# One decoder layer on one core: the program's work in program order, weight splits in pieces between matmul groups, attention over the full array

## The chip, the cores and the metric

The kernel runs on one core of a Trainium2 chip. A core has a matrix engine (TensorE, PE in the profile; its weight loads are shown as PEld), three engines for elementwise work (VectorE or DVE, ScalarE or ACT, GpSimd or POOL) and queues that issue DMAs, most of them on SyncE (SP). Each engine has its own stream of instructions, and waits on semaphores that others raise.

The metric is the time of one execution on the device in microseconds; lower is better. Three runs of the kernel before gave a median of 829.25 us (828.92 to 829.86).

## What is computed

One layer with 512 tokens of width 1024 and a memory of 256 rows, in float32. Each of three parts adds a normalised result to `x`:

```python
# 1. mixer: one input projection, 8 attention heads of 64 and 4 retention heads of 128
proj = rms_norm(x, pre_mix_g) @ w_in                     # 1024 -> 3584
a = dilated_attention(rope(aq), rope(ak), av)            # windows (128,1) (512,4) (2048,16)
a = a * rsqrt(mean(a * a) + eps) * attn_gn_g             # per head
r = retention(rope(rq), rope(rk) * 128 ** -0.5, rv)      # chunks of 128, decay by head
r = silu(rg) * (groupnorm(r) * ret_gn_g)
x = x + rms_norm(concat(a, r) @ w_out, post_mix_g)
# 2. cross attention on the memory, 4 heads of 256
q = rms_norm(x, pre_mem_g) @ w_q;  k, v = split(rms_norm(mem, mem_norm_g) @ w_kv)
x = x + rms_norm(softmax(q @ k.T / 16) @ v @ w_o, post_mem_g)
# 3. feed-forward, hidden 2816
g, u = split(rms_norm(x, pre_ffn_g) @ w_gate_up)
x = x + rms_norm((silu(g) * u) @ w_down, post_ffn_g)
```

## The kernel before

**Products.** Almost every product is made of three (`mm3`, lines 81 to 86): each operand is held as a high part rounded to TensorE's fast 32-bit format and the rest as a low part, and high x high, high x low and low x high are summed in PSUM. `split` (line 88) makes the two parts: ScalarE copies the high one, VectorE subtracts it for the low one.

**Weights.** They come in 67 blocks of 128 x 2048 (1 MB) in a fixed order: 14 of `w_in`, 8 of `w_kv`, 4 each of `w_out`, `w_q` and `w_o`, 22 of `w_gu` (gate and up), 11 of `w_dn`. `load` takes the next: a buffer `raw` (two of them), the DMA on SP's queue, then the split in halves of 1024 columns into `wh` and `wl`. `take` hands out a block and loads one or two ahead.

**Stages.** Queries and keys of the retention are projected feature by feature (`rqk`, eight PSUM banks at once) and rotated; then values and gate (`rv`, `rg`) block by block of tokens; then attention queries, keys and values (`aq`, `ak`, `av`) mixed with the retention's heads (`ret_inner`, `ret_state`, `ret_outer`). The eight attention heads follow: scores (`att_scores`, masked by a table that holds the logarithm of how often the three patterns see a key), transposes of the weights (`att_transposes`), values (`att_values`), a norm for each pair of heads (`att_norm`), with the projections of the memory (`mem_keys`, `mem_values`) as filler between them. Then the output projection (`mix_half`), the cross attention, its output projection by blocks of tokens (`mem_block`), gate and up (22 steps of 48 matmuls of 512 columns), and the down projection with the last residual.

**Order.** The kernel is written for a library that assigns buffers and semaphores. Without further options it also orders each engine's instructions itself, by priority and readiness. An instruction waits for the producers of what it reads, and for the readers of a buffer that it takes over.

In the scores, the first product of each pair holds all 128 rows of the array (`qk` holds a query's high half above its low half), the second only the 64 rows of the head, for the keys' low part:

```python
            nc.tensor.matmul(ps, lhsT=c, rhs=qk[pr][:, (2 + hh) * S:(2 + hh) * S + nn], start=True, stop=False)
            nc.tensor.matmul(ps, lhsT=c[rows], rhs=kl[rows, pr * S:pr * S + nn], start=False, stop=True)
```

The attention's values are products in full float32 with 64 output columns: four for a head, the two heads of a pair in the two halves of one bank.

Of the kernel before, what the change touches and what calls it, by code (L numbers as in the profile page):

```python
# [19 lines left out]
P = 128  # L20
# [18 lines left out]
def hybrid_layer(ctx, tc, t, out):  # L39
    nc = tc.nc  # L40
    cp = ctx.enter_context(tc.tile_pool(name="cp", bufs=1))
    up = ctx.enter_context(tc.tile_pool(name="up", bufs=20))
# [23 lines left out]
    def row(name):  # L66
        return wk.tile([P, D], F32, tag="w4k", name=uname(name), bufs=2)
# [31 lines left out]
    loaded = {}  # L99

    def load(pieces=1, swap=False):
# [3 lines left out]
        w = pair("w")  # L105
        n = 2048 // pieces
        for i in range(pieces):
            c = slice(i * n, (i + 1) * n)
            nc.sync.dma_start(raw[:, c], src[:, c])
        n = 2048 // max(2, pieces)  # L110
        for i in range(max(2, pieces)):
            c = slice(i * n, (i + 1) * n)
            if swap and i == 0:
                nc.vector.tensor_copy(w[0][:, c], raw[:, c])
                nc.vector.tensor_sub(w[1][:, c], raw[:, c], w[0][:, c].bitcast(F32))
            else:
                split(raw[:, c], w[0][:, c], w[1][:, c])
        loaded[key] = w

    def take(name, i, ahead=2):  # L120
        while (name, i) not in loaded:
            load()
        while chunks and len(loaded) - 1 < ahead:
            load()
        return loaded.pop((name, i))

    def ahead(name, i):
        while (name, i) in chunks:
            load()
# [35 lines left out]
    def load_gain(name):  # L165
        g = wk.tile([P, D], F32, tag="g", name=uname("g"), bufs=2)
        src = t[name]
        nc.sync.dma_start(g, bass.AP(tensor=src.tensor, offset=src.offset, ap=[[0, P], [1, D]]))
        return g
# [17 lines left out]
    def load_xT(k, between=None):  # L187
        raw = work("xraw")
        nc.sync.dma_start(raw, t["xT"][:, k, :])
        if between:  # L190
            between()
        split(raw, *hx(k, 0, S), gT[:, 0, k:k + 1])
# [6 lines left out]
    load_xT(0, lambda: load(4, True))  # L199
    load_xT(1)  # L200
    load_xT(2)
    load_xT(3)
    load(2)
    for k in range(4, KT):
        load_xT(k)
    load()
    x = load_rows("x")
    load()
    w_rqk = [take("w_in", i, 0) for i in range(4)]
    rope = unit("rope").rearrange("p (c s) -> p c s", c=4)  # L210
    nc.sync.dma_start(rope, t["rope"])
# [6 lines left out]
    pss = [bank("rqk") for _ in range(8)]  # L218

    def rqk(f, k):  # L220
        w = w_rqk[k // 2]
        mm3(pss[f], part(w, (k % 2) * D + f * P, P), hx(k, 0, S), k == 0, k == KT - 1)

    for k in range(4):
        for f in range(8):
            rqk(f, k)
    ahead("w_in", 4)
    rstd0 = row_rstd(x, TB, D, "r0")
    rbc = None
    for f in range(8):  # L230
        for k in range(4, KT):
            rqk(f, k)
        ps = pss[f]
# [19 lines left out]
    def tok_proj(c0, name, evict):  # L253
        ws = []

        def one(b):
            if b == 0:
                ws[:] = [take("w_in", c0, 1), take("w_in", c0 + 1, 2)]
# [3 lines left out]
            if b == TB - 1:  # L262
                ws.clear()
            evict(b, ps)
# [39 lines left out]
    off = [0, 512, 1024, 896]  # L304
# [64 lines left out]
    qk = [unit("qk", F32R) for _ in range(4)]  # L369
    kl = unit("kl", F32R)  # L370
    av = unit("av")
# [8 lines left out]
    def split_k(f, v):  # L380
        for i, (h, g) in enumerate(((ha, hb), (hb, ha))):
            o = qk[f][:, (2 + i) * S:(3 + i) * S]
            nc.scalar.copy(o[h], v[h])
            nc.vector.tensor_sub(kl[h, f * S:(f + 1) * S], v[h], o[h].bitcast(F32))
            nc.scalar.copy(o[g], o[h].bitcast(F32))

# [10 lines left out]
    def head_proj(c0, store, name):  # L397
        ws = {}

        def one(f):  # L400
# [4 lines left out]
            for k in range(KT):  # L405
                mm3(ps, part(w, k * 256 + (f % 2) * P, P), hx(k, 0, S), k == 0, k == KT - 1)
            t1, t2 = work("t1"), work("t2")
# [9 lines left out]

    def evict_av(b, ps):
        nc.scalar.mul(av[:, b * 512:(b + 1) * 512], ps, rstd0[:, b:b + 1])

# [7 lines left out]
    def att_scores(h):  # L428
        pr, hh = h // 2, h % 2
        rows = slice(hh * 64, hh * 64 + 64)  # L430
# [7 lines left out]
        for qb in (3, 2, 0, 1):  # L438
# [3 lines left out]
            ps = bk[sbank[qb][0]][:, sbank[qb][1]:sbank[qb][1] + nn]  # L442
            nc.tensor.matmul(ps, lhsT=c, rhs=qk[pr][:, (2 + hh) * S:(2 + hh) * S + nn], start=True, stop=False)
            nc.tensor.matmul(ps, lhsT=c[rows], rhs=kl[rows, pr * S:pr * S + nn], start=False, stop=True)
# [11 lines left out]

    def att_transposes(h):
        pt = pts.pop(h)
        u = unit("pT")
        bk = [bank("ptr") for _ in range(3)]  # L460
        for kb in (0, 1, 3, 2):
            ps = bk[off[kb] // 512]
            for qb in range(kb, TB):
                o = off[kb] % 512 + (qb - kb) * P
                nc.tensor.transpose(ps[:, o:o + P], pt[:, poff[qb] + kb * P:poff[qb] + (kb + 1) * P], ident)
        nc.scalar.copy(u[:, 0:512], bk[0])
        nc.vector.tensor_copy(u[:, 512:1024], bk[1])
        nc.scalar.copy(u[:, 1024:1280], bk[2][:, :256])
        pTs[h] = u

    def att_values(h):
        pr, hh = h // 2, h % 2
        rows = slice(hh * 64, hh * 64 + 64)
        if hh == 0:
            oTb[pr] = bank("oT")
        u = pTs.pop(h)
        for kb in range(TB):
            nc.tensor.matmul(oTb[pr][rows, kb * P:S], lhsT=av[:, kb * 512 + h * AD:kb * 512 + (h + 1) * AD],
                             rhs=u[:, off[kb]:off[kb] + S - kb * P], start=kb == 0, stop=kb == TB - 1)
        if hh == 1:  # L480
            ot = work("ot")
            nc.scalar.copy(ot, oTb.pop(pr))
            oTb[pr] = ot
# [27 lines left out]
    mem = {}  # L511

    def mem_prepare():
        raw = rawp.tile([P, KT, NM], F32, tag="raw", name=uname("memTr"))
# [7 lines left out]
    def mem_stats():  # L522
        mrow = rawp.tile([P, 2, D], F32, tag="raw", name=uname("mrow"))
# [5 lines left out]
    def mem_keys(f):  # L529
        if f % 2 == 0:  # L530
            mem["w"] = take("w_kv", f // 2, 1)
        ps = bank("mk")
        for k in range(KT):
            mm3(ps[:, :NM], part(mem["w"], k * 256 + (f % 2) * P, P), part(mem["T"], k * NM, NM), k == 0, k == KT - 1)
        kf = work("kf")
# [5 lines left out]
    def mem_values(c, b):  # L541
        if b == 0:
            mem["w"] = [take("w_kv", 4 + 2 * c + i, i) for i in range(2)]
        ps = bank("mv")
        for k in range(KT):
            mm3(ps, part(mem["T"], k * NM + b * P, P), part(mem["w"][k // 4], (k % 4) * 512, 512), k == 0, k == KT - 1)
        vf = work("vf")
        nc.scalar.mul(vf, ps, mem["r"][:, b:b + 1])
        hi, lo = part(mem["v"], b * D + c * 512, 512)
        nc.scalar.copy(hi, vf)  # L550
        nc.gpsimd.tensor_sub(lo, vf, hi.bitcast(F32))
# [49 lines left out]
    x = load_rows("x")  # L601
    g1 = load_gain("post_mix_g")
# [8 lines left out]
    ahead("w_out", 2)  # L611
    filler(9)
    att_out(3)
    w_out = {c: take("w_out", c, 0) for c in (2, 3, 0, 1)}

    def residual(pss, b, g, e=None, cuts=((0, 512), (512, 512))):
        e = e or nc.vector
        ss = small([P, len(cuts)], "ps")
        z = row("z")
# [12 lines left out]
    def normed(b, g, e=None):  # L632
        rs = row_rstd([x[b]], 1, D, "nr", e=e)
        h = row("h")
# [14 lines left out]
    def out_proj(bs, lhs, ws, ks, name, outer, mid=None):  # L649
# [11 lines left out]
        for b in bs:  # L661
            for n in range(2):
                if mid and (b, n) == (bs[-1], 1 if len(bs) == 1 else 0):
                    mid()
                for i in range(2 * outer, KT):
                    one(b, n, i)
        return pss
# [4 lines left out]
    g2 = load_gain("pre_mem_g")  # L672
# [3 lines left out]
    def mix_half(hf, mid=None):  # L676
        bs = (2 * hf, 2 * hf + 1)
        pss = out_proj(bs, y_lhs, w_out, order, "o1", 2, mid)
        hs = []
        for b in bs:  # L680
            e = nc.gpsimd if b == 3 else nc.vector
            residual(pss[b], b, g1, e)
            hs.append(normed(b, g2, e))
# [11 lines left out]
    wq = [take("w_q", c, 0) for c in range(4)]  # L695
    qT, pT, oT = {}, {}, {}

    def query(hf, f):
# [3 lines left out]
        for k in range(KT):  # L702
            mm3(ps[:, :256], part(wq[f // 2], k * 256 + (f % 2) * P, P), part(h2[hf], k * 256, 256), k == 0, k == KT - 1)
# [270 lines left out]
```

## Time and profile before

| what | value |
|---|---|
| median of three runs | 829.25 us |
| the profiled execution, first to last instruction | 828.5 us |
| its mean granted TensorE clock | 0.991 |
| DMA | 85.86 MB, mean 104 GB/s |
| HBM read, written | 83.11 MB, 2.10 MB |

Busy time of an engine is the union of its instructions. A matmul's row is longer than the distance to the next one, since its end is modelled and matmuls are pipelined; the distance between starts is what it takes of TensorE. The granted clock is the share of full speed that TensorE had. "Idle before" is the engine's idle time ahead of an instruction, and the arrow names what ended it. The page's chain covers 42% of the span with TensorE's matmuls, the down projection's and gate/up's groups at 5% each.

### The profile page before, as it was taken

To read this page: it belongs to the slowest core of one execution; us is meant where nothing else is said; L and a number is where in the kernel's file an instruction comes from. 1 tells how busy PE (TensorE), PEld (TensorE's weight loads), DVE (VectorE), ACT (ScalarE), POOL (GpSimd) and SP (SyncE) were. 2 spreads that over 40 slices of the span, in tenths; PEclk is the share of its full clock that TensorE was granted. 3 is DMA by queue.
4 is the path that set the end of the run, shared out by engine and by line. 5 is a ranking of instruction groups with operands and counts; after the bars stand their busy time and mean duration, and the time that the engine had idled before them with its cause. 6 is when DMAs were issued, how large, how long until landed. Compare 5 with 4: busy or idle time off the path is not lost. (4 is left out here: it accounts for less than half of the span.)

```text
span 828.5 us, 10220 instructions
## 1 busy us (share of the span) xinstructions
PE 807.9 (98%) x4108; PEld 675.7 (82%) x4108; DVE 396.6 (48%) x766; ACT 305.4 (37%) x537; POOL 132.8 (16%) x176
## 2 busy tenths in 40 slices
PE   9979999999999999999999899999999999999996
PEld 7768888877777878999988788888888888888884
DVE  5595168764565657758446441405050314222144
ACT  5504333466464733445435232222130305332110
POOL 0161024410110100300036300000000004236000
PEclk9998999999999999999999999999999999999998
DMA  8726212221124440524002340505050322521011
GB/s 305 291 77 236 94 51 87 73 95 52 51 70 175 163 153 0 197 109 153 1 1 102 127 153 1 203 1 203 1 203 1 121 82 74 182 102 51 1 51 51
DMA packets 15519, 85.86 MB, mean 104 GB/s; under 512 B 1904, under 2 KB 1904, under 8 KB 6896
## 3 DMA queue, kind: packets, MB, share of 16 engines
q1 hardware_dynamic: 14752, 84.16, 27.7%
q10 hardware_dynamic: 720, 1.06, 0.3%
q8 instruction: 32, 0.52, 0.3%
q14 instruction: 15, 0.12, 0.0%
HBM read 83.11 MB, written 2.10 MB: 103 GB/s over the span
## 5 line engine op out<-in xcount | busy, mean ns | idle before, releaser
L91 DVE TENSOR_TENSOR wl<-raw,wh 128x1024 fp32r<-128x1024 f32 (+1 forms) x135 | 166.5, 1267 | 102.6 <-ACT wh L90 70.2
L90 ACT CAST wh<-raw 128x1024 fp32r<-128x1024 f32 (+1 forms) x135 | 133.8, 1042 | 95.3 <-DMA raw<-in_w_in 38.1
L820 DVE TENSOR_TENSOR af<-sg,u 128x512 f32<-128x512 f32 x22 | 15.1, 686 | 133.7 <-PE u L86 133.7
L846 POOL TENSOR_TENSOR al<-af,ah 128x512 fp32r<-128x512 f32 x22 | 34.6, 1605 | 257.5 <-ACT ah L845 243.3
L84 PE MATMUL g<-h3h,wh 128*128 128x512 f32 (+1 forms) x192 | 72.1, 375 | 0.0
L84 PE MATMUL u<-h3h,wh 128*128 128x512 f32 (+1 forms) x192 | 71.7, 373 | 0.0
L85 PE MATMUL g<-h3l,wh 128*128 128x512 f32 (+1 forms) x192 | 71.3, 371 | 0.0
L86 PE MATMUL g<-h3h,wl 128*128 128x512 f32 (+1 forms) x192 | 71.3, 371 | 0.0
L85 PE MATMUL u<-h3l,wh 128*128 128x512 f32 (+1 forms) x192 | 71.3, 371 | 0.0
L86 PE MATMUL u<-h3h,wl 128*128 128x512 f32 (+1 forms) x192 | 71.3, 371 | 0.0
L84 PE MATMUL dn<-wh,ah 128*128 128x512 f32 x176 | 68.5, 389 | 0.0
L85 PE MATMUL dn<-wl,ah 128*128 128x512 f32 x176 | 68.5, 389 | 0.0
L86 PE MATMUL dn<-wh,al 128*128 128x512 f32 x176 | 68.5, 389 | 0.0
L817 ACT ACTIVATE sg<-g 128x512 f32<-128x512 f32 x22 | 13.1, 598 | 149.2 <-PE g L86 123.0
L84 PEld LDWEIGHTS g<-h3h,wh 128*128 128x128 f32 x192 | 36.5, 190 | 6.5 <-ACT h3h L90 0.2
L84 PEld LDWEIGHTS u<-h3h,wh 128*128 128x128 f32 x192 | 36.6, 191 | 6.3
L85 PEld LDWEIGHTS g<-h3l,wh 128*128 128x128 f32 x192 | 36.2, 188 | 6.4
L86 PEld LDWEIGHTS g<-h3h,wl 128*128 128x128 f32 x192 | 36.2, 188 | 6.2
L85 PEld LDWEIGHTS u<-h3l,wh 128*128 128x128 f32 x192 | 36.2, 188 | 6.2
L86 PEld LDWEIGHTS u<-h3h,wl 128*128 128x128 f32 x192 | 36.1, 188 | 6.1
L84 PEld LDWEIGHTS dn<-wh,ah 128*128 128x128 f32 x176 | 33.0, 188 | 6.9
L86 PEld LDWEIGHTS dn<-wh,al 128*128 128x128 f32 x176 | 33.0, 188 | 6.9
(267 smaller groups left out, 1752.8 us busy)
## 6 DMA issues: line engine op xcount, KB each, us to landing
raw<-in_w_gu SPq DMA_DIRECT2D x22, 1024.0 KB, 4.8
raw<-in_w_in SPq DMA_DIRECT2D x12, 1024.0 KB, 5.1
raw<-in_w_dn SPq DMA_DIRECT2D x11, 1024.0 KB, 4.7
raw<-in_w_kv SPq DMA_DIRECT2D x8, 1024.0 KB, 4.7
x<-in_x SPq DMA_DIRECT2D x4, 1024.0 KB, 10.2
raw<-in_w_out SPq DMA_DIRECT2D x4, 1024.0 KB, 5.3
raw<-in_w_q SPq DMA_DIRECT2D x4, 1024.0 KB, 5.3
raw<-in_w_o SPq DMA_DIRECT2D x4, 1024.0 KB, 4.7
```

Source lines behind the costliest of these rows:

```text
L84: nc.tensor.matmul(o, lhsT=sh, rhs=mh, start=start, stop=False)
L85: nc.tensor.matmul(o, lhsT=sh, rhs=ml, start=False, stop=False)
L86: nc.tensor.matmul(o, lhsT=sl, rhs=mh, start=False, stop=stop)
L90: nc.scalar.copy(hi, src)
L91: nc.vector.tensor_sub(lo, src, hi.bitcast(F32))
L817: nc.scalar.activation(sg, pg, AF.Silu)
L820: nc.vector.tensor_mul(af[-1][:, (f % 4) * S:(f % 4 + 1) * S], sg, pu)
L846: nc.gpsimd.tensor_sub(lo[:, c], af[i][:, c], hi[:, c].bitcast(F32))
```

## The change

- **Program order.** `TileContext` gets `linearize=True`. The instructions then stand on each engine in the order in which the code issues them.
- **Weights in pieces.** `load` becomes `fetch` (the DMA alone) and `piece` (one half of 1024 columns: ScalarE's high part, the low part on VectorE, or on GpSimd for the first halves of `w_kv` and `w_out`). The piece that completes a block also fetches the next. `bg` makes a piece if fewer than `ahead` blocks are ready, and stands in the code behind a matmul group and ahead of its eviction.
- **Start.** The transposed input and the first blocks of `w_in` are fetched and split between the groups of `rqk`.
- **Retention rotation.** ScalarE copies the two halves of the product in swapped places into `t2`, VectorE multiplies all 128 rows at once; before, VectorE multiplied each half into the other's place. The table's signs are exchanged to fit.
- **Attention.** The keys' low parts are held in both halves of the rows (one more copy, on GpSimd), so the second product of the scores uses all 128 rows. The transposed weights are split into high and low parts; the values are held as high and low parts side by side, 128 columns for a head; eight products in the fast format replace the four, and ScalarE and VectorE add the two halves of the result.
- **Buffers.** 23 units in place of 20; rows and gains come from units; a smaller scratch area for DMA descriptors.
- **Smaller ones.** `mem_values` takes one block at a time and keeps two banks; the memory's rows come into units; the last block of `mem_block` computes its norms on VectorE.

```diff
-    up = ctx.enter_context(tc.tile_pool(name="up", bufs=20))
+    up = ctx.enter_context(tc.tile_pool(name="up", bufs=23))
...
+    def fetch(pieces=1):
+        if not chunks:
+            return
         key = chunks.pop(0)
         src = t[key[0]][key[1]]
         raw = rawp.tile([P, 2048], F32, tag="raw", name=uname("raw"))
...
+    def piece(n=1024, first=False):
...
+        key, raw, w, c0 = e
+        c = slice(c0, c0 + n)
+        if first:
+            nc.vector.tensor_copy(w[0][:, c], raw[:, c])
+        else:
+            nc.scalar.copy(w[0][:, c], raw[:, c])
+        low = nc.gpsimd if key[0] in ("w_kv", "w_out") and c0 == 0 else nc.vector
+        low.tensor_sub(w[1][:, c], raw[:, c], w[0][:, c].bitcast(F32))
+        e[3] += n
+        ready[key] = w
+        if e[3] == 2048:
+            fetched.pop(0)
+            fetch()
+        return True
+
+    def bg(n=1, ahead=2):
+
+        for _ in range(n):
+            if fetched and (len(ready) - (fetched[0][0] in ready) < ahead):
+                piece()
...
+        nc.scalar.copy(t2[0:64], ps[64:128])
+        nc.scalar.copy(t2[64:128], ps[0:64])
         nc.vector.tensor_mul(t1, ps, rope[:, 0, :])
-        nc.vector.tensor_mul(t2[0:64], ps[64:128], rope[64:128, 1, :])
-        nc.vector.tensor_mul(t2[64:128], ps[0:64], rope[0:64, 1, :])
+        nc.vector.tensor_mul(t2, t2, rope[:, 1, :])
         nc.gpsimd.tensor_add(dst, t1, t2)
...
+            k0 = (pr % 2) * 2 * S + hh * S
             nc.tensor.matmul(ps, lhsT=c, rhs=qk[pr][:, (2 + hh) * S:(2 + hh) * S + nn], start=True, stop=False)
-            nc.tensor.matmul(ps, lhsT=c[rows], rhs=kl[rows, pr * S:pr * S + nn], start=False, stop=True)
+            nc.tensor.matmul(ps, lhsT=c, rhs=kl[pr // 2][:, k0:k0 + nn], start=False, stop=True)
...
+        for i, (c0, n) in enumerate(((0, 512), (512, 384), (1024, 384))):
+            split(bk[i][:, :n], hi[:, c0:c0 + n], lo[:, c0:c0 + n])
...
+        for kb, (c0, n, q0) in enumerate(pcol):
+            for i in range(2):
+                nc.tensor.matmul(ps[:, q0:q0 + n], lhsT=av_block(kb, h, 1), rhs=u[i][:, c0:c0 + n],
+                                 start=kb == 0 and i == 0, stop=kb == TB - 1 and i == 1)
         if hh == 0:
-            oTb[pr] = bank("oT")
...
+            oTb[pr] = work("ot")
+        ol = work("ol")
+        nc.scalar.copy(ol[ha], ps[hb])
+        nc.vector.tensor_add(oTb[pr][rows], ps[ha], ol[ha])
...
         for j, ps in enumerate((pg, pu)):
             for k in range(KT):
                 mm3(ps[:, c0:c0 + n], part(w, k * 256 + j * P, P), gx(k, c0, n), k == 0, k == KT - 1)
+            bg(1)
...
-    nc = _bacc.Bacc("TRN2", target_bir_lowering=False, num_devices=1)
+    nc = _bacc.Bacc("TRN2", target_bir_lowering=False, num_devices=1, dynamic_dma_scratch_size=1024)
...
-    with _tile.TileContext(nc) as tc:
+    with _tile.TileContext(nc, linearize=True) as tc:
```

How the instructions stand in the built programs, with the semaphores that each waits for (named by the engine or DMA queue that raises them), at three places.

ScalarE before, in the gate/up stage (`wh` is a weight block's high part, `sg` the gate after its activation):

```order
L90 CAST wh_4926<-raw_4925 128x1024 [waits DMAHW2_49]
L90 CAST wh_4926<-raw_4925 128x1024
L817 ACTIVATE sg_4922<-g_4872 128x512 [waits DVE_49,PE_49,Activation_49]
L90 CAST wh_4987<-raw_4986 128x1024 [waits DMAHW3_49]
L90 CAST wh_4987<-raw_4986 128x1024
L90 CAST wh_5048<-raw_5047 128x1024 [waits DMAHW4_49]
L90 CAST wh_5048<-raw_5047 128x1024
L817 ACTIVATE sg_4983<-g_4933 128x512 [waits DVE_49,PE_49]
```

The same place after the change:

```order
L127 CAST wh_5008<-raw_4915 128x1024 [waits PE_49] x2
L883 ACTIVATE sg_5040<-g_4982 128x512 [waits DMAHW2_49,DVE_49]
L127 CAST wh_5069<-raw_4976 128x1024 [waits PE_49] x2
L883 ACTIVATE sg_5101<-g_5043 128x512 [waits DMAHW3_49,DVE_49]
L127 CAST wh_5130<-raw_5038 128x1024 [waits PE_49] x2
L883 ACTIVATE sg_5162<-g_5104 128x512 [waits DMAHW4_49,DVE_49]
```

Before, the casts wait for their block's DMA and the activation for its matmuls. After, each cast waits for TensorE, which it doesn't read, and the activation for VectorE and for a DMA: that of the block that the piece ahead of it in the code has just fetched. Both casts of a block stand between two activations.

SyncE after the change, in the same stage:

```order
L112 DMA raw_4976<-in_w_gu 128x2048 [waits DMAHW7_49,DVE_49]
L112 DMA raw_5038<-in_w_gu 128x2048 [waits DMAHW0_49,DVE_49]
L112 DMA raw_5099<-in_w_gu 128x2048 [waits DMAHW1_49,DVE_49]
L112 DMA raw_5160<-in_w_gu 128x2048 [waits DMAHW2_49,DVE_49]
L112 DMA raw_5221<-in_w_gu 128x2048 [waits DMAHW3_49,DVE_49]
```

Each fetch waits for VectorE: the low half that stands ahead of it in the code. Its own semaphore is the one that the activation above waits for.

TensorE before, in the attention (scores `s`, values `oT` with the transposed weights `pT`):

```order
L443 MATMUL s_1947<-qk_686 128x512 [waits DVE_49]
L444 MATMUL s_1947<-kl_687,qk_686 128x512
L443 MATMUL s_1948<-qk_686 128x384 [waits PE_49]
L444 MATMUL s_1948<-kl_687,qk_686 128x384
L443 MATMUL s_1949<-qk_686 128x256 [waits DVE_49]
L444 MATMUL s_1949<-kl_687,qk_686 128x256
L443 MATMUL s_1949<-qk_686 128x256
L444 MATMUL s_1949<-kl_687,qk_686 128x256
L478 MATMUL oT_1967<-pT_1862,av_688 64x512 [waits Activation_49]
L478 MATMUL oT_1967<-pT_1862,av_688 64x384 [waits DVE_49]
L478 MATMUL oT_1967<-pT_1862,av_688 64x256 [waits Activation_49]
L478 MATMUL oT_1967<-pT_1862,av_688 64x128
```

After the change, a head's values and the transposes behind them:

```order
L532 MATMUL oT_1844<-pTh_1704,av_693 128x512 [waits PE_49,Pool_49]
L532 MATMUL oT_1844<-pTl_1705,av_693 128x512
L532 MATMUL oT_1844<-pTh_1704,av_693 128x384
L532 MATMUL oT_1844<-pTl_1705,av_693 128x384
L532 MATMUL oT_1844<-pTh_1704,av_694 128x256
L532 MATMUL oT_1844<-pTl_1705,av_694 128x256
L532 MATMUL oT_1844<-pTh_1704,av_694 128x256
L532 MATMUL oT_1844<-pTl_1705,av_694 128x256
L517 MATMUL ptr_1859<-ident,p_1669 128x128 [waits DVE_49]
```

Eight products of 128 output columns stand for the four of 64. The first waits for GpSimd, whose instruction ahead of it in the code belongs to the memory's keys; the transposes, which read `p`, wait for VectorE, which stands ahead of them in the code with the sum of the values.

Counted over the whole built program: in the order of the code, 1,244 neighbouring instructions stand on different engines (DMA issues included), and 1,235 of the later ones wait for the earlier one's semaphore at the count that its end, or its landing, brings. In the program before, of 2,480 such neighbours 9 do.

More of the change, by code (lines that the diff above doesn't have):

```diff
@@ L104, in load, with take @@
         raw = rawp.tile([P, 2048], F32, tag="raw", name=uname("raw"))
-        w = pair("w")
         n = 2048 // pieces
         for i in range(pieces):
[L108 to L129, printed above, removed]
+            nc.sync.dma_start(raw[:, i * n:(i + 1) * n], src[:, i * n:(i + 1) * n])
+        fetched.append([key, raw, None, 0])
+    def piece(n=1024, first=False):
+        if not fetched:
+            return False
+        e = fetched[0]
+        if e[2] is None:
+            e[2] = pair("w")
+        key, raw, w, c0 = e
[16 more added lines that the diff above has]
+                piece()
+    def take(name, i):
+        key = (name, i)
+        while key not in ready or (fetched and fetched[0][0] == key):
+            assert piece()
+        return ready.pop(key)
     def rsqrt(v, n, name, e=None):
@@ L694, in hybrid_layer @@
     w_out.clear()
-    wq = [take("w_q", c, 0) for c in range(4)]
+    wq = [take("w_q", c) for c in range(4)]
     qT, pT, oT = {}, {}, {}
```

215 lines of the change are left out of this document (123 added, 92 removed).

## The prediction

> **What bounds the kernel now.** I read the page first: the busy shares, then the slices.
>
> ```profile
> span 828.5 us, 10220 instructions
> ...
> PE 807.9 (98%) x4108; PEld 675.7 (82%) x4108; DVE 396.6 (48%) x766; ACT 305.4 (37%) x537; POOL 132.8 (16%) x176
> ...
> PE   9979999999999999999999899999999999999996
> ...
> PEclk9998999999999999999999999999999999999998
> ```
>
> TensorE is busy in every slice at nearly full clock. The other three together are busy for 834.8 us, as much as the whole span, and all of it lies beside matmuls. The waits say how little TensorE waits:
>
> ```profile
> PE rv L85 <- DVE wl L91: 5.2, 1, 5.2
> PE tp L792 <- DVE h L635: 4.0, 1, 4.0
> PE warm L215 <- POOL ones L196: 1.0, 1, 1.0
> PE bc L176 <- DVE diag L175: 0.9, 2, 0.6
> ```
>
> With five shorter ones they add to 12 us. What an idle TensorE pays afterwards stands in the timeline behind the first of them, and in three windows (busy us and count of PE, PEld, DVE, ACT, POOL; granted clock; DMA share; GB/s):
>
> ```profile
> 62.09 0.79 PE L85 MATMUL rv<-wl,hTh 128*128 128x512 f32 x1 [5.16 <-DVE wl L91]
> ...
> 65.67 0.63 PE L84 MATMUL rv<-wh,hTh 128*128 128x512 f32 x1
> 66.09 0.48 PE L85 MATMUL rv<-wl,hTh 128*128 128x512 f32 x1
> 66.41 0.39 PE L86 MATMUL rv<-wh,hTl 128*128 128x512 f32 x1
> 66.64 0.39 PE L85 MATMUL rv<-wl,hTh 128*128 128x512 f32 x1
> ```
>
> ```profile
> 60.00:80.00 20.00, 17.91 (x70) 14.69 (x71) 12.79 (x12) 7.74 (x9) 2.31 (x1) 0.84 0.64 236
> 460.00:480.00 20.00, 15.98 (x119) 15.41 (x118) 6.88 (x9) 7.99 (x11) 3.71 (x14) 0.91 0.24 102
> 500.00:520.00 20.00, 20.00 (x90) 16.57 (x89) 4.55 (x5) 4.72 (x6) 0.00 (x0) 1.00 0.00 1
> ```
>
> Matmuls start 0.42 us apart (65.67 to 66.09) until the clock comes back, then 0.23 us apart (66.41 to 66.64), though each row's length is 0.39: an end lies 0.16 us behind the next start. Four us at half clock cost 4.0 x (1 - 0.227/0.427) = 1.9 us. In the second window a clock of 0.91 is 3.6 us at half speed, 1.7 us lost. I take **1.8 us for each long idle time**, on top of the idle time itself.
>
> **What the change does to that.** Its words say that each engine keeps program order. The built program says more: at 1,235 of the 1,244 places where program order passes from one engine to another, the later instruction waits for the earlier one to end; before, at 9 of 2,480. A weight fetch waits for the instruction ahead of it, and the next one waits until the fetch has landed. So nothing lies beside anything else: the program is one chain, and what was cover becomes length. The forecast is the sum of the chain.
>
> The end of the kernel before is already such a chain, and prices its steps:
>
> ```profile
> 820.28 0.39 PE L86 MATMUL dn<-wh,al 128*128 128x512 f32 x1
> 820.76 0.60 ACT L624 ACTIVATE junk<-dn 128x512 bf16<-128x512 f32 x1 [4.75 <-PE dn L86]
> 821.26 0.19 ACT L624 ACTIVATION_READ_ACCUMULATOR junk<-dn 128x1 f32 x1
> 821.48 0.21 DVE L625 TENSOR_SCALAR pv<-ps,pv 128x1 f32<-128x1 f32 x1 [4.69 <-ACT junk L624]
> ...
> 824.13 1.42 DVE L630 SCALAR_TENSOR_TENSOR x<-z,pry,x 128x512 f32<-128x512 f32 x2
> 824.91 0.33 SPq L877 DMA_DIRECT2D out<-x  x1
> ```
>
> TensorE to ScalarE takes 0.09 us (820.67 to 820.76), ScalarE to VectorE 0.03 (821.45 to 821.48): about 0.05 us per handover, besides the 0.16 us of the last matmul's end.
>
> *TensorE.* Packed matmuls: 828.5, less 12 of waits, 7.8 behind the last matmul (820.67 to the end) and 3.6 of half clock, is 805 us. The attention becomes shorter:
>
> ```profile
> 197.17 0.28 PE L86 MATMUL mk<-memTh,wl 128*128 128x256 f32 x1
> 197.29 0.28 PE L84 MATMUL mk<-memTh,wh 128*128 128x256 f32 x1
> ...
> 199.81 0.39 PE L443 MATMUL s<-qk 128*128 128x512 f32 x1
> 200.13 0.50 PE L444 MATMUL s<-kl,qk 64*128 64x512 f32 x1
> ...
> 202.56 2.37 PE L478 MATMUL oT<-pT,av 128*64 128x512 f32 x8
> 204.85 1.31 PE L465 MATMUL ptr<-ident,p 128*128 128x128 f32 x10
> ```
>
> A head's scores alternate 128 and 64 rows of the array and take 2.75 us (199.81 to 202.56); its values, half the columns and full-precision operands, take 2.29 us (to 204.85). At the packed pitch (0.12 us for 256 columns, 0.23 for 512, 0.17 between) eight full-array matmuls of 512, 384, 256 and 256 columns, each twice, take 1.27 us. That saves 1.5 + 1.0 us a head, 20 us for eight: 785 us. No row has a 64-row stream without alternation, so the gain from the scores lies between 0 and 12 us; beside the rest it does not matter. PE work comes in 252 runs with something else between: 252 x 0.16 = 40 us of ends. **825.**
>
> [...]
>
> *VectorE, ScalarE, GpSimd* go onto the path whole:
>
> ```profile
> L91 DVE TENSOR_TENSOR wl<-raw,wh 128x1024 fp32r<-128x1024 f32 (+1 forms) x135 | 166.5, 1267 | 102.6 <-ACT wh L90 70.2
> L90 ACT CAST wh<-raw 128x1024 fp32r<-128x1024 f32 (+1 forms) x135 | 133.8, 1042 | 95.3 <-DMA raw<-in_w_in 38.1
> L820 DVE TENSOR_TENSOR af<-sg,u 128x512 f32<-128x512 f32 x22 | 15.1, 686 | 133.7 <-PE u L86 133.7
> L846 POOL TENSOR_TENSOR al<-af,ah 128x512 fp32r<-128x512 f32 x22 | 34.6, 1605 | 257.5 <-ACT ah L845 243.3
> ...
> L817 ACT ACTIVATE sg<-g 128x512 f32<-128x512 f32 x22 | 13.1, 598 | 149.2 <-PE g L86 123.0
> ```
>
> VectorE: 12 low halves go to GpSimd (12 x 1.27 = -15) and the rotation has 8 operations fewer (-5); 24 low parts of the transposed weights, 8 additions and 4 low parts of the values come (about 0.6 us each by the 512-wide row, +22): 398. Operations that ran into each other (135 x 1.267 is 171, busy is 166.5) now stand apart: **410.** ScalarE: 16 half-height copies for the rotation at about 0.6 (row of sg), wider high parts and the values' copies, +18; apart, +10: **333.** GpSimd: 12 x 2 x 1.605 = 38 for the low halves, 8 half-height copies between nothing and 1.6 each (I take 1.2), 16 small fills at 0.2: **180.**
>
> *DMA.* All landing times come onto the path:
>
> ```profile
> raw<-in_w_gu SPq DMA_DIRECT2D x22, 1024.0 KB, 4.8
> ...
> out<-x SPq DMA_DIRECT2D x4, 256.0 KB, 2.0
> ...
> g<-in_post_mem_g SPq DMA_DIRECT2D x1, 512.0 KB, 3.7
> ```
>
> 65 weight blocks and 7 other megabytes at 4.8 (346), 6 of half a megabyte near 3.7 (22), some 20 smaller ones between 2.0 and 2.5 and the two blocks that come in pieces (59): **427.** The x loads took 10.2 us before, with other loads in flight; alone I give them 4.8.
>
> [...]
>
> *Handovers:* 1,244 x 0.05 = **62.**
>
> Sum: 825 + 410 + 333 + 180 + 427 + 62 = **2,237 us** at full clock.
>
> *Clock.* By the same durations 119 of the 252 runs stand behind more than 3.4 us of idle TensorE: in the gate/up stage, behind each up group, 1.04 + 1.27 + 4.8 + 0.6 + 0.69. 47 of them last over 4 us and lose 1.8 us each (85), 27 last 1.9 to 4 us and lose 1.7 (46), 45 shorter ones (38 us of work) run at half speed whole (33): 164 us. The 97 runs behind 1.2 to 3.4 us (cast and low half, 2.3 us) lie between no loss and the full price, 129 us; no row shows such a gap, so I take half. **+230.** The ends are 0 and 785 x 0.88 = 690.
>
> [...]
>
> So 2,237 + 230 = 2,467, and with the 0.75 us between the profiled span and the median of the runs (829.25) **2,468 us, three times the time before.** What hid every edit is the other engines' running beside TensorE; with that gone there is no later limit that could give it back.
>
> **Rivals.**
>
> *Engines in order, but side by side* (faster). Then the matmuls stay packed: 829.3 - 20 of attention, less the 5.2 + 1.9 us of the rv wait, which pieces between groups take away, and the 4.0 + 1.7 us of the tp wait, whose norm goes to VectorE: **796 us.** For it: the other engines have the room (48, 37 and 16%). Against it: the waits in the built program, where a matmul group waits for a product that it doesn't read. It decides while TensorE idles less than 33 / 252 = 0.13 us before each run; one cast and one subtraction are 2.3.
>
> *Fetches awaited at issue only.* Then 427 shrinks to 103 x 0.33 = 34 and fewer gaps are long (clock about +190): **2,035 us.** Against it: the waits are on the DMA queues' semaphores.
>
> *Clock never, or always, at half:* **2,237 or 2,930 us.** The two stretches above speak against never; 87 runs of over 5 us, in which the clock comes back within 4, against always.
>
> **How the numbers follow.** One chain with the clock between: 0.82, time 2,468. Clock always at half or near it: 0.06; never: 0.03. Fetches at issue only: 0.05. Side by side: 0.04, of which 0.01 is eaten to within 0.2%, about what a measurement of this kernel tells from no change. The range takes in half to double the clock's term (2,350 to 2,700) and some 60 us for means taken under other neighbours: **2,290 to 2,700.** Faster 0.03, same 0.01, slower 0.96.
>
> **What would show it.** In the profile after: TensorE, VectorE, ScalarE and GpSimd busy one at a time (shares of about 43, 17, 14 and 7%, DMA the rest); every gate/up step some 24 us, 11 of it matmuls; granted clock between 0.5 and 0.9 in nearly every slice; a matmul group that starts 0.05 us behind the end of the ScalarE, VectorE or GpSimd instruction ahead of it in the code; mean traffic near 35 GB/s. The attention's rows should show 8 scores in about 1.3 us where the clock is full. Wrong would be: a PE share over 60%, weight fetches that run under matmuls, or handovers well off 0.05 us, since there are 1,244 of them.

## The result, and the profile after

The changed kernel takes 2,570.38 us (2,569.64 to 2,570.75, four runs) against 829.56 us for the kernel before on the same chip: a ratio of 3.098, 95% interval 3.093 to 3.102. The forecast was 2,468 us in a range of 2,290 to 2,700. Direction, mechanism and range held; the value is 102 us short.

The page of the changed kernel, with busy shares and slices:

```profile
span 2568.7 us, 10390 instructions
...
PE 1163.9 (45%) x4108; PEld 917.0 (36%) x4108; DVE 415.5 (16%) x793; ACT 347.1 (14%) x565; POOL 136.9 (5%) x193
...
PE   1344453333433433434274345446565656445534
PEclk9566776566655555666586566767777777777767
```

TensorE was busy for 9 tenths of nearly every slice; now it is for 3 to 6 tenths of most. The four engines' busy times add to 2,063 us, and by the starts and ends in the trace at least one of them is busy for 2,060 us of the 2,569: they no longer overlap. Before, they added to 1,643 us in a span of 828.5. The clock line, nearly all 9 before, is 5 to 7 in 38 of the 40 slices.

One gate/up step in the timeline (only rows that begin a run of an engine are kept, and the fetch), with the idle time of each engine and what ended it:

```profile
2004.99 1.04 ACT L127 CAST wh<-raw 128x1024 fp32r<-128x1024 f32 x1 [7.08 <-PE u L87]
2006.07 1.23 DVE L129 TENSOR_TENSOR wl<-raw,wh 128x1024 fp32r<-128x1024 f32 x1 [6.90 <-ACT wh L127]
2007.32 0.33 SPq L112 DMA_DIRECT2D raw<-in_w_gu  x1
2012.12 0.60 ACT L883 ACTIVATE sg<-g 128x512 f32<-128x512 f32 x1 [6.08 <-DMA raw<-in_w_gu]
2012.75 0.69 DVE L886 TENSOR_TENSOR af<-sg,u 128x512 f32<-128x512 f32 x1 [5.45 <-ACT sg L883]
...
2013.49 0.80 PE L85 MATMUL g<-h3h,wh 128*128 128x512 f32 x1 [8.54 <-DVE af L886]
...
2021.39 1.04 ACT L127 CAST wh<-raw 128x1024 fp32r<-128x1024 f32 x1 [8.68 <-PE g L87]
2022.47 1.23 DVE L129 TENSOR_TENSOR wl<-raw,wh 128x1024 fp32r<-128x1024 f32 x1 [9.03 <-ACT wh L127]
...
2023.75 0.50 PE L85 MATMUL u<-h3h,wh 128*128 128x512 f32 x1 [2.39 <-DVE wl L129]
```

Each row starts within 0.1 us of the end of the instruction ahead of it, shown or left out, but for `sg`, which waits until the fetch has landed. This ScalarE activation reads only `g`, whose group had ended some 15 us earlier (a cast behind it ended 7.08 us before 2004.99), and yet waits for a weight block that it never touches: 4.8 us from the fetch's issue (2007.32) to its start (2012.12). The matmul group at 2013.49 waits for a product (`af`) that it doesn't read. That is the chain, as forecast.

The clock in the same step, in windows of 3.41 us that begin where the granted clock changes (busy us and count of PE, PEld, DVE, ACT, POOL; granted clock; DMA share; GB/s):

```profile
2007.79:2011.20 3.41, 0.00 (x0) 0.00 (x0) 0.00 (x0) 0.00 (x0) 0.00 (x0) 0.50 0.79 281
2011.20:2014.62 3.42, 1.13 (x3) 0.94 (x4) 0.69 (x1) 0.60 (x1) 0.00 (x0) 0.50 0.06 26
2014.62:2018.03 3.41, 3.41 (x10) 2.64 (x9) 0.00 (x0) 0.00 (x0) 0.00 (x0) 0.50 0.00 0
2018.03:2021.44 3.41, 3.33 (x15) 2.39 (x13) 0.00 (x0) 0.05 (x1) 0.00 (x0) 1.00 0.00 0
2021.44:2024.86 3.42, 1.11 (x5) 0.94 (x6) 1.23 (x1) 1.00 (x1) 0.00 (x0) 1.00 0.00 0
2024.86:2028.27 3.41, 3.41 (x10) 2.63 (x9) 0.00 (x0) 0.00 (x0) 0.00 (x0) 0.50 0.00 0
2028.27:2031.69 3.42, 2.82 (x13) 2.00 (x11) 0.00 (x0) 0.56 (x1) 0.00 (x0) 1.00 0.00 0
```

Read from the top: the gate group starts at 2013.49 inside a window at half clock. That window is a third busy, so the next one is at half as well; only after this one, busy throughout, does full speed come back. The gate group spent 4.5 us at half speed. Then a gap of only 2.4 us (2021.39 to 2023.75) leaves one window a third busy, and the next, wholly busy one, is at half speed again. The count over all windows of the trace: of 483 at half clock, none of the 352 that were under three quarters busy was followed by full clock, all 116 that were over 85% busy were, and 3 of the 15 between. Of 249 at full clock, 130 of the 131 that were at least 45% busy kept it, and none of the 118 less busy ones did.

### The profile page after: what moved, and what is told of

Read it like the earlier page. It is cut to its first block, busy times and chain, and to the rows that moved or that the text cites. A ratio compares the mean times of both kernels' runs of the same rounds, so it can differ in the third digit from the quotient of the medians.

```text
span 2568.7 us, 10390 instructions
## 1 busy us (share of the span) xinstructions
PE 1163.9 (45%) x4108; PEld 917.0 (36%) x4108; DVE 415.5 (16%) x793; ACT 347.1 (14%) x565; POOL 136.9 (5%) x193
## 5 line engine op out<-in xcount | busy, mean ns | idle before, releaser
L129 DVE TENSOR_TENSOR wl<-raw,wh 128x1024 fp32r<-128x1024 f32 (+1 forms) x124 | 149.8, 1208 | 1109.4 <-ACT wh L127 1109.4
L85 PE MATMUL g<-h3h,wh 128*128 128x512 f32 (+1 forms) x192 | 98.5, 513 | 186.8 <-DVE af L886 172.0
L85 PE MATMUL rqk<-hTh,wh 128*128 128x512 f32 x64 | 40.9, 639 | 113.2 <-POOL rkT L287 24.4
L86 PE MATMUL g<-h3l,wh 128*128 128x512 f32 (+1 forms) x192 | 91.1, 475 | 0.0
L87 PE MATMUL g<-h3h,wl 128*128 128x512 f32 (+1 forms) x192 | 89.9, 468 | 0.0
L85 PE MATMUL q<-hhh,wh 128*128 128x256 f32 x128 | 44.7, 349 | 69.3 <-DMA raw<-in_w_o 42.7
L912 POOL TENSOR_TENSOR al<-af,ah 128x512 fp32r<-128x512 f32 x22 | 27.8, 1261 | 809.6 <-ACT ah L911 737.1
L85 PEld LDWEIGHTS rqk<-hTh,wh 128*128 128x128 f32 x64 | 19.4, 303 | 128.1 <-issue 40.8
L85 PE MATMUL o<-wh,yTh 128*128 128x512 f32 x64 | 30.8, 482 | 62.5 <-DMA raw<-in_w_q 30.0
L85 PEld LDWEIGHTS q<-hhh,wh 128*128 128x128 f32 x128 | 31.2, 244 | 73.1 <-issue 50.3
L86 PEld LDWEIGHTS g<-h3l,wh 128*128 128x128 f32 x192 | 51.7, 269 | 9.4
```

Of the source, the lines that this page charges most:

```text
L85: nc.tensor.matmul(o, lhsT=sh, rhs=mh, start=start, stop=False)
L86: nc.tensor.matmul(o, lhsT=sh, rhs=ml, start=False, stop=False)
L87: nc.tensor.matmul(o, lhsT=sl, rhs=mh, start=False, stop=stop)
L129: low.tensor_sub(w[1][:, c], raw[:, c], w[0][:, c].bitcast(F32))
L912: nc.gpsimd.tensor_sub(lo[:, c], af[i][:, c], hi[:, c].bitcast(F32))
```

## The experiments

All ratios are against runs of the kernel before on the same chip. Its median was 829.4 to 830.9 us on the chips used, so times of different runs can be set side by side within about 2 us. In the tables, PE busy is TensorE's busy time in the profiled execution, and the rest of the span is what is left beside it, both in us; clock is the mean granted clock.

**1. The order without the waits, and the waits without the order.** The first kernel keeps every engine's instructions in the changed kernel's order, but has no waits beyond those for data and buffers:

```diff
-    with _tile.TileContext(nc, linearize=True) as tc:
+    with _tile.TileContext(nc) as tc:
         hybrid_layer(tc, aps, out)
+        last = {}
+        for i in list(nc.cur_bb.bb.instructions):
+            if i.engine in last:
+                tc.add_manual_dep(i, last[i.engine].name, mybir.DependencyInfo(
+                    mybir.DependencyClass.NoSync, mybir.DependencyReason.DATA), reason="order")
+            last[i.engine] = i
```

> The changed kernel with every engine's instructions in exactly the same order as in it, but without the waits for the instruction ahead on another engine (order only, no landing or end awaited that the data do not need). Theory A (the one chain is the waits, and the order costs nothing): the engines run side by side again, 796 us as worked out in the prediction, up to 850 if some engine's queue now holds a late step ahead of an early one; mean clock 0.97 or more. Theory B (the order written out is itself the cause, because an engine's queue is blocked by its own earlier work): 1,300 us or more. Between 850 and 1,300 both have a share.

The second only drops `linearize=True`, so that the library orders each engine's work:

> The changed kernel with only the argument that serialises it taken out: each engine's order is then chosen by the scheduler, as in the kernel before. Theory A: 790 to 835 us, no more than 3% from e1_same_order_no_waits. Theory B: as the kernel before less 20 us for attention (809), but well below e1_same_order_no_waits, by more than 20%.

The third is the kernel before with `linearize=True`:

> The kernel before, unchanged but for the argument that serialises it. Theory A with the clock as the trace of the changed kernel shows it (windows of 3.41 us; half speed ends only after a window that was nearly all busy, full speed ends after a window less than half busy): the sum of this kernel's chain is 2,157 us at full clock (PE 784 with the old attention, DMA 420, DVE 413, ACT 323, POOL 106, ends 32, handovers 79), and its 195 matmul runs lose 225 us to the clock: 2,382 us, clock near 0.66. With the clock as the prediction had it (1.8 us for each gap over 3.4 us, half of that for 1.2 to 3.4) the loss is 158 and the time 2,315. Theory B: 830 to 900 us.

| kernel | us | ratio (95%) | PE busy | rest of the span | clock |
|---|---|---|---|---|---|
| before | 829 to 831 | 1 | 807.9 | 20.6 | 0.991 |
| changed order, no waits (e1) | 890.13 | 1.071 (1.070 to 1.073) | 808.6 | 79.9 | 0.957 |
| free order (e2) | 829.61 | 0.998 (0.998 to 0.999) | 793.5 | 33.9 | 0.984 |
| before in one chain (e3) | 2420.36 | 2.914 (2.910 to 2.919) | 1063.6 | 1349.4 | 0.713 |

So the waits alone triple the time of either kernel, and the order alone costs 7%. Theory A's own upper end (850) was missed by e1, and so were its clock of 0.97 and its 3% between e1 and e2: the order is not free. Theory B's 1,300 us for e1, and its 900 at most for e3, are far off.

e3 took 105 us more than by the prediction's clock rule (2,315), and 38 more than by the windows (2,382). Of these 38, which are 31 in the profiled execution, 10 are clock (235 for 225), 8 ScalarE (331 for 323) and 13 TensorE at full clock (829 for 784 and 32 of ends): the expectation had put the matmuls with the old attention at 784, where the prediction's own count was 805.

The idle time of TensorE in e1 stands in its longest waits:

```profile
PE bc L197 <- DVE diag L196: 16.3, 6, 9.5
PE ptr L517 <- DVE pTl L92: 10.7, 1, 10.7
PE o L85 <- DVE oTxl L92: 6.2, 1, 6.2
PE otr L545 <- DVE ot L538: 5.3, 4, 2.5
```

All four are waits for VectorE, which is held to the written order; in sum it is busy for 413.7 us of 888.5, so its results come late though it is far from full. From 828.5 to 888.5, 20 us of attention go and 59 outside TensorE's busy time come; of the 21 that remain, 17 are the clock, since TensorE was busy for 45 us at half clock in e1 and for 8 before.

**2. What breaks cost.** By the windows counted above, the clock's price should depend on how often matmuls are broken, and not on how long TensorE is idle in all. Two kernels, still one chain, with the same instructions in fewer runs. In the first, `bg` does nothing, so that a block is split whole when it is taken:

```diff
-        for _ in range(n):
-            if fetched and (len(ready) - (fetched[0][0] in ready) < ahead):
-                piece()
+        return
```

> The changed kernel, still one chain, with no pieces of weight splits between matmul groups: both halves of a block are split together when the block is taken. The same instructions, 205 matmul runs in place of 252. By the clock's windows as read off the changed kernel's trace: 108 us less clock loss and 11 us less of ends and handovers, 2,451 us. By the prediction's rule (1.8 us per long gap, half for short ones): 53 and 11 us less, 2,506. If clock loss followed the idle time alone, which is the same but for those ends: 2,559.

In the second, both pieces of a gate/up step stand behind its two groups:

```diff
             for k in range(KT):
                 mm3(ps[:, c0:c0 + n], part(w, k * 256 + j * P, P), gx(k, c0, n), k == 0, k == KT - 1)
-            bg(1)
+        bg(2)
```

> The changed kernel, still one chain, with the two pieces behind each gate/up block's matmuls instead of one behind the gate group and one behind the up group: the same instructions, 229 matmul runs in place of 252, so 23 long runs in place of 46. By the clock's windows: 42 us less clock loss and 6 us less of ends and handovers, 2,522 us. By the prediction's rule (1.8 us per gap over 3.4 us, half for shorter ones): 21 and 6 us less, 2,543. If the loss follows idle time alone: 2,564.

e4 took 2,474.82 us (ratio 2.978, 2.973 to 2.983), e8 2,533.87 (3.054, 3.049 to 3.059): 96 and 37 us less than the changed kernel. Each time lies between the value from the windows and the one from the prediction's rule: e4 24 us above the first and 31 below the second, e8 12 above and 9 below, so that e8's time alone doesn't tell them apart. Idle time alone (2,559 and 2,564) is out. The clock's loss itself can be read from each trace: the length of every matmul run less its matmuls at the packed distances and 0.16 us of end. Beside it what each rule gives for that kernel (for the windows, a sum in time with the clock of each window set by how busy the one before was; the rule was read off the changed kernel alone):

| kernel | matmul runs | prediction's rule | windows | measured |
|---|---|---|---|---|
| changed | 252 | 232 | 356 | 346 |
| before in one chain (e3) | 195 | 158 | 225 | 235 |
| no pieces between (e4) | 205 | 179 | 248 | 255 |
| one run per block (e8) | 229 | 211 | 313 | 317 |

The windows are within 10 us in all four; the prediction's rule is 76 to 114 short in all. In e3, 20 us are taken off for the older, slower attention. The busy lines, first of e3, then of e4:

```profile
PE 1063.6 (44%) x4108; PEld 832.2 (34%) x4108; DVE 414.0 (17%) x766; ACT 330.9 (14%) x537; POOL 106.1 (4%) x176
```

```profile
PE 1065.0 (43%) x4108; PEld 855.4 (35%) x4108; DVE 415.3 (17%) x793; ACT 347.2 (14%) x565; POOL 137.3 (6%) x193
```

Some 99 us of TensorE's time went between the changed kernel and e4 (1,163.9 to 1,065.0), 91 of them clock and 8 the ends of 47 runs; VectorE, ScalarE and GpSimd stayed within 0.4 us. The line of e3 prices what a chain does to the old instructions, and comes back below.

With engines side by side the same edit does the opposite. The free-order kernel e2, with `bg` empty:

> e2_order_free (the changed kernel with the scheduler's order) with no pieces of weight splits between matmul groups. Theory F (the pieces, written between groups, put weight splits ahead of the evictions that TensorE waits for on VectorE, and so eat what attention and rotation give): 812 to 818 us. Rival (the pieces cost nothing where engines run side by side; what is eaten goes to other edits): 828 to 832.

874.14 us (ratio 1.055, 1.053 to 1.057), slower than e2 by 45. Both expectations fell: the pieces are neither harmful there nor free, they are what hides the splits.

```profile
PE q L85 <- ACT wh L127: 9.5, 2, 5.2
PE g L87 <- DVE wl L129: 7.3, 6, 1.7
PE rqk L85 <- ACT wh L127: 5.4, 1, 5.4
PE av L85 <- ACT wh L127: 4.9, 1, 4.9
```

Without them TensorE waits for splits at the moment a block is taken.

**3. The parts of the change by themselves, in the kernel before.**

> The kernel before with the full-array scores and values of the change alone (21 buffers of 8 KB in place of 20, which the low parts of the values need). Theory C (from the trace of e2_order_free: TensorE gains the 20 us that the prediction gave the attention, 1.5 us a head in the scores and 1.0 in the values, and VectorE, which gets 24 low parts of transposed weights, 4 of the values and 8 additions in that stage, gives 10 to 15 back): 815 to 825 us, with TensorE waits behind VectorE's av or pTl rows that the kernel before has not. Theory D (the attention is worth its 20 us by itself, and e2_order_free lost them to its other edits): 808 to 813 us. Theory E (nothing gained): 829 or more.

> The kernel before with the full-array scores alone (the second half of the low parts of the keys filled by GpSimd; values as before). Theory C: 8 x 1.5 = 12 us less on TensorE and nothing more on VectorE, so all of it stays: 817 to 821 us. Theory D: 817 to 821 as well, but then e5_full_attention_alone is 8 us below it; by theory C e5_full_attention_alone is not below this kernel by more than 3. Theory E: 829 or more.

> The kernel before with the retention rotation swapped through ScalarE alone. Theory: hidden beside TensorE, within 0.2% of the kernel before (829 to 833), since VectorE gives 5 us and ScalarE takes 10 in a stage where TensorE waits for neither. Rival: the copies on ScalarE hold up the casts of the weights behind them, and the wait of rv for wl grows from 5.2 us: 833 to 840.

Their edits are those of the diff (`att_scores`, `att_transposes`, `att_values`, `evict_av` and `split_k` for e5; `att_scores` and `split_k` for e6; the four lines of the rotation and its table for e7).

| kernel | us | ratio (95%) | PE busy | rest of the span |
|---|---|---|---|---|
| full attention (e5) | 819.57 | 0.987 (0.986 to 0.989) | 791.4 | 26.2 |
| full scores (e6) | 823.78 | 0.993 (0.991 to 0.994) | 795.9 | 24.9 |
| rotation (e7) | 822.81 | 0.992 (0.990 to 0.993) | 807.4 | 15.2 |

On TensorE the scores are worth just what the prediction took them for, 8 x 1.5 = 12.0 us (807.9 to 795.9), and e2's rows show one head at full clock, scores, values and the transposes behind them:

```profile
212.03 0.40 PE L493 MATMUL s<-qk 128*128 128x512 f32 x1
212.26 0.40 PE L494 MATMUL s<-kl,qk 128*128 128x512 f32 x1
212.50 0.33 PE L493 MATMUL s<-qk 128*128 128x384 f32 x1
212.67 0.34 PE L494 MATMUL s<-kl,qk 128*128 128x384 f32 x1
212.85 0.28 PE L493 MATMUL s<-qk 128*128 128x256 f32 x1
...
213.32 0.40 PE L532 MATMUL oT<-pTh,av 128*128 128x512 f32 x1
...
214.62 1.25 PE L517 MATMUL ptr<-ident,p 128*128 128x128 f32 x10
```

Full-array matmuls follow each other at 0.23 and 0.17 us on the same rows. The scores take 1.29 us (212.03 to 213.32) and the values 1.30 (to 214.62), for 2.75 and 2.29 before: 1.5 and 1.0 us a head, as forecast. Not all of it reaches the end: the rest of the span grows by 4 us in e6 and 6 in e5. In e5 the new waits cost clock too: TensorE was busy for 17 us at half clock, for 8 before, which takes another 4 of the 20 us. The longest wait that the kernel before has not, of e5:

```profile
PE s L453 <- DVE av L428: 2.8, 1, 2.8
```

and the two longest such of e6:

```profile
PE s L445 <- ACT av L421: 1.8, 1, 1.8
PE oT L481 <- ACT pT L469: 1.5, 1, 1.5
```

Theory C named VectorE for e5, and there the waits are `s` for `av` (the attention's values) and `mk` and `otr` for `ot` (the attention's result; 2.5 us together). In e6, where C expected nothing to be given back, TensorE now comes early for two ScalarE evictions. C is right on e5 and wrong on e6, and e5 is 4 us below e6, more than C's 3. Theory D (808 to 813 for e5) is out.

The rotation was expected to be hidden, or by the rival to cost time, and is a gain of 6.6 us: both fell. The longest waits of the kernel with the rotation alone (`tp` are the transposes of the normed rows `h` ahead of gate/up):

```profile
PE tp L793 <- DVE h L636: 4.0, 1, 4.0
PE warm L215 <- POOL ones L196: 1.0, 1, 1.0
```

The 5.2 us in which `rv` waited for `wl` are gone. The timeline of VectorE shows why, first of the kernel before:

```profile
59.39 0.69 DVE L246 TENSOR_TENSOR t<-rqk,rope 64x512 f32<-64x512 f32 x1
60.09 0.68 DVE L247 TENSOR_TENSOR t<-rqk,rope 64x512 f32<-64x512 f32 x1
60.81 5.71 DVE L91 TENSOR_TENSOR wl<-raw,wh 128x1024 fp32r<-128x1024 f32 x4
```

and of the rotation alone:

```profile
48.60 1.37 DVE L248 TENSOR_TENSOR t<-t,rope 128x512 f32<-128x512 f32 x1
49.89 1.21 DVE L91 TENSOR_TENSOR wl<-raw,wh 128x1024 fp32r<-128x1024 f32 x1
51.03 0.68 DVE L247 TENSOR_TENSOR t<-rqk,rope 128x512 f32<-128x512 f32 x1
51.63 1.18 DVE L248 TENSOR_TENSOR t<-t,rope 128x512 f32<-128x512 f32 x1
52.73 1.21 DVE L91 TENSOR_TENSOR wl<-raw,wh 128x1024 fp32r<-128x1024 f32 x1
```

Before, 24 operations of the rotation stood in one piece (40.73 to 60.77) ahead of four low halves of weights; now there are 16, one pair waits 2.4 us for ScalarE's copies (ahead of 46.69), and low halves stand between the pairs, the first of them 11 us earlier (49.89 for 60.81). The prediction had counted the 5 us that VectorE saves, but not whom it frees: it gave the end of that wait to the pieces (in its side-by-side rival).

**4. The parts that pay, together.**

> The kernel before with two parts of the change, the full-array attention and the rotation through ScalarE, and its own scheduling. If the two gains lie in different stages (rotation: the wait of rv for wl; attention: scores and values) they add: 829.4 - 9.9 - 6.6 = 813 us, and the wait of rv is gone from the trace. If they share VectorE's or ScalarE's slack: 816 to 820.

> e9_attention_and_rotation with the last residual and norm of the memory stage on VectorE in place of GpSimd, and three gate/up blocks in place of two begun on the first half of the columns before its transposes. If the 4.0 us wait of tp for h is covered by the third block (2.8 us of matmuls), and its half clock goes with it: 4.0 + 1.8 less, 807 us. If VectorE's queue of weight splits holds the norm up as long as GpSimd's slower operations did: 812 to 814.

```diff
-        residual(out_proj((b,), o_lhs, wo, nat, "o2", 0, mid)[b], b, g3, nc.gpsimd)
-        return normed(b, g4, nc.gpsimd)
+        e = nc.vector if b == TB - 1 else nc.gpsimd
+        residual(out_proj((b,), o_lhs, wo, nat, "o2", 0, mid)[b], b, g3, e)
+        return normed(b, g4, e)
...
-    for f in range(2):
+    for f in range(3):
```

812.32 us (0.978, 0.977 to 0.980) and **806.44 us** (0.972, 0.970 to 0.973). The two gains add, and the last step brings 5.9 us where 5.8 were worked out for it: in e9 `tp` still waits 4.2 us for `h`; in e10 the longest wait left is 2.4. The first rows of e9's waits, and the first of e10's:

```profile
PE tp L808 <- DVE h L651: 4.2, 1, 4.2
PE s L454 <- DVE av L429: 2.4, 1, 2.4
```

```profile
PE s L454 <- DVE av L429: 2.4, 1, 2.4
```

The step holds two edits, VectorE for the last norm and the third block; what each of them brings wasn't tried.

So e10 is 2.8% faster than the kernel before. Why e2, with the same attention and rotation, ends 17 us above e9 isn't settled: its span has 13 us more outside TensorE's busy time than the kernel before, and its seven longest waits are all for VectorE (of `rv`, `s`, `tp`, `bc` and `ptr`). At their head:

```profile
PE rv L86 <- DVE wl L129: 5.4, 3, 3.2
PE s L493 <- DVE av L468: 4.9, 1, 4.9
```

Which of the other edits brings them wasn't tried one by one. The wait of `rv` for `wl`, gone in e7, is back here in three parts, though this kernel has the same rotation.

## Why the prediction was right, and where its sum was off

**The mechanism was right.** One chain, from the waits of the built program; e3 shows that they alone do it, and e1 that without them the same order is at 890. The rival of fetches awaited at issue only (2,035) is out: nothing but a DMA was under way for 419 us of the span, and the ScalarE row above waits for a landing. The two rivals on the clock (2,237 and 2,930) are out as well: the windows above change between 0.50 and 1.00, and the loss lies between none and the 690 us of a clock that is always at half.

The terms, in us:

| term | forecast | measured |
|---|---|---|
| TensorE at full clock, ends included | 825 | 818 |
| clock | 230 | 346 |
| VectorE | 410 | 415 |
| ScalarE | 333 | 347 |
| GpSimd | 180 | 137 |
| DMA alone under way | 427 | 419 |
| nothing busy (handovers) | 62 | 87 |
| sum | 2,467 | 2,569 |

The terms that came out longer add to 160 us, those that came out shorter to 58. That the value is only 102 us short is thus in part luck.

**The clock is the term that was mis-sized**, by 116 us, more than the whole miss. Two steps of it failed. "I take 1.8 us for each long idle time" rested on two stretches, 4.0 and 3.6 us at half speed; in the changed kernel half speed ended only after a window of 3.41 us that was at least three quarters busy (none of 352 below that), and by this a run that begins anywhere in a window would have about one to two windows of it, if it lasts that long. The 40 runs of 4 to 6 us (at full clock) behind gaps over 3.4 us spent 3.2 to 6.0 us at half speed and lost 2.36 us each, and all runs behind such gaps 208 in place of 164. "I take half" of 129 for the gaps of 1.2 to 3.4 us: 110 were lost, nearly the full price. The gap of 2.4 us in the timeline left a window a third busy (1.11 of 3.42 us), and a window at half speed followed. The 37 runs behind still shorter gaps, which the prediction gave nothing, lost 28. The borders at 1.2 and 3.4 us of idle time, on which the forecast of 230 was built, were the author's assumption: the two waits read in the kernel before were 5.2 and 4.0 us long, and no run shows a border in idle time at either length. In the trace the clock follows how busy the window of 3.41 us ahead was.

**GpSimd** was 43 us too dear. The prediction used rows of a kernel in which other engines worked beside it. The low halves of the weights and those of the activations, after:

```profile
L129 POOL TENSOR_TENSOR wl<-raw,wh 128x1024 fp32r<-128x1024 f32 x12 | 28.1, 2338 | 211.5 <-ACT wh L127 169.9 <-issue 41.6
L912 POOL TENSOR_TENSOR al<-af,ah 128x512 fp32r<-128x512 f32 x22 | 27.8, 1261 | 809.6 <-ACT ah L911 737.1 <-issue 72.5
```

The second took 1,605 ns before and takes 1,261 alone (1,262 in e3, with the old order). The 12 low halves of weights took 2.34 us each, not 3.21. Of the 43 us, 27 are old instructions that run shorter alone (132.8 to 106.1 in e3) and 16 the change's own work (31 for 47). That work is 28.1 us of low halves for a forecast 38, 4.9 of copies for 9.6 and 3.3 of fills, less 5.3 for the last block's norms, which went to VectorE and stand in no item of the prediction. Its items add to 184 us; the 180 that went into the sum is a slip.

**Handovers** came out at 0.07 us (87 over 1,244) for 0.05, worth 25 us. ScalarE is 14 us over: its old instructions, which the prediction lengthened by 10 us when they no longer run into each other, take 25 more in e3 (305.4 to 330.9), and the new ones 16 for 18. The other terms lie within 8 us. A gate/up step takes 26.3 us (2013.49 to 2039.75) for a forecast 24. Its matmuls take 15.3 us for 11 at full clock, so some 4 us are the clock; the 24 held about 2 of it beside 22 us of matmuls, splits, landing, activation and product. Handovers well off 0.05 us were one of the prediction's signs of being wrong; 0.07 is 40% more, and the chain stays the same.

**The attention** was sized right on TensorE (e6, and e2's rows), and the prediction's remark that the scores' gain lies between 0 and 12 us is settled at 12. In the changed kernel itself it can't be seen: all eight heads' scores run at half clock there, 2.7 us each from the first start to the last end.

**The side-by-side rival** was priced too low. The prediction gave 796 us to engines in order but without waits; e1 is 890. It counted the other engines' free time in sum (48, 37 and 16% busy) and not what stands ahead of whom in VectorE's queue.

## What to carry to other kernels

Ahead of any sum, look in the built program at what each first instruction behind a change of engine waits for: here waits for something it doesn't read turned cover into length, 2,420 us for 830 by them alone (e3). Where TensorE is broken into short runs as here, price the clock by windows and by the number of runs, and not by the sum of idle time: the windows came within 10 us of the measured loss in four kernels, and joining two groups into one run saved 37 us with the same work (e8). A low share of busy time on an engine didn't tell when its results came: VectorE was busy for 414 of 888 us in e1, and the four longest waits of TensorE were for it. Taking 5 us off VectorE ahead of one late operand was worth 6.6 us (e7), more than half of the 9.9 that the attention's rewriting brought (e5).

## What was not expected of the hardware

In the changed kernel full clock was lost after a window of 3.41 us that was less than about 45% busy, not only after an idle one (118 of 118, against 1 of 131 above that), and came back after every one that was over 85% busy (116 of 116) and after few below (3 of 15 down to 75%, none of 352 under that). The other kernels in one chain place the first border less sharply: in e4 7 of the 11 windows that were 45 to 50% busy lost full clock, in e3 7 of 14. Five windows of e3, all between 616 and 760 us of its span, fit neither border. An operation of GpSimd with two inputs ran 21% shorter in the mean, 1,261 for 1,605 ns, when no other engine ran: before, 15 of the 22 took 1.28 to 1.30 us and 7 took 2.26 to 2.28, after, all took 1.26. What made those 7 longer wasn't tried. A weight block of a megabyte landed in 4.7 us alone, about the same as beside matmuls before (4.8).
